# A nineteenth home for expert weights: the residual rows wait in DRAM while the experts run

## The chip, the cores and the metric

One core of one Trainium2 chip runs the whole program. The metric is device microseconds of one execution, the median of several. A profiled execution takes some microseconds longer than an unprofiled one; both times are given below. TensorE multiplies matrices, VectorE, ScalarE and GpSimd (in the profile DVE, ACT and POOL) do the rest on tiles in SBUF, and 16 DMA engines move data between DRAM and SBUF. A DMA is issued by an instruction on one of three queues: SyncE's (SP), ScalarE's (ACT) or GpSimd's (POOL). SP does nothing else here.

## The reference

256 tokens of 1024 features pass through three blocks. The first is attention and a gated convolution, and then a mixture of experts; the second and third are a gated delta rule and a forgetting attention, which are not touched by the change. What matters is the middle of the first block:

```
x = x + gt1 * y                        # residual rows, 256 x 1024 fp32 = 1 MB
h = rmsnorm(x, norm2_g) * (1 + sc2) + sh2
x = x + gt2 * hierarchical_moe(h, ...) # 32 experts, each token goes to 2 of them
x = rmsnorm(x, final_norm_g)           # and on into the second block
```

An expert has a gate and an up matrix of 1024 x 128 and a down matrix of 128 x 1024, fp32, 0.5 MB each. All 32 are read from DRAM whatever the routing: 48 MB.

## The kernel before

**Residual rows.** The tile `x` (128 partitions, 2 halves of the tokens, 1024 features; 1 MB) lives in the pool `res`. Its last writers ahead of the experts are four pieces of the output projection, `w2(0)` to `w2(3)` (line 1133), each for 256 columns: VectorE multiplies and adds (lines 1138, 1139), ScalarE squares for the norm (line 1140). After that `x` is read a last time for the routing side: TensorE transposes it (line 690), GpSimd copies columns 0 to 95 of every 128 (line 1598) and ScalarE the other 32 (line 1605) into `xp`. Nothing reads or writes `x` again until `join` (line 1877), where VectorE adds the experts' sum to it (line 1887).

**Experts.** `moe` (line 1497) splits them into eight quads of four. A quad has six loads of 1 MB: four with gate and up of one expert (two DMAs of 0.5 MB, lines 1529 and 1530), two with down of two experts (line 1536; line 1532 for the last quad). So there are 48 loads, number 6q to 6q+5 for quad q. All are issued on SP, in an order that is written out by hand. Each needs a home, a tile of 1 MB. There are 18 of them, listed in `ECYC` (line 1312): five tiles of the pool `rg` (r0 to r4), four `raw` and four `hl` tiles of the pool `wp`, and five of the block's own pool. Loads 0 to 17 get them in list order; they are issued in the order `EFIRST`, from the time when the tiles' earlier users are done, while the output projection still runs. From then on a counter walks round the list: load 18 gets the home of load 0, and so on. Two of its turns go to the gate/up and down weights of one extra tile of 32 slots, step 8 of `order`, which takes tokens that overflow their expert's 32 slots.

**Steps.** `moe_loop` (line 1747) takes the quads in the order 0, 1, 2, 3, extra, 4, 5, 6, 7, as steps i = 0 to 8. In a step `s1(i)` multiplies with gate and up (line 1333), `turn(i)` transposes, `s2(i)` multiplies with down (line 1359), and `s3(i)` adds to the sums in PSUM (lines 1377, 1378). `ahead(q)` issues the six loads of quad q some steps before they are used: quad 3 after s2(0), quads 6 and 7 after s2(4) and s2(5). SP waits in order until the home of the next load is free, that is until the matmuls that read the home's last load are done; so `s1(0)` and `s2(0)` free the homes for quad 3.

**After the experts.** `gdn` (line 1999) queues on SP, right behind the last expert load: `gfin` (0.5 MB), a weight piece `raw`, two tiles `adaA` (each 1 MB), another `raw`, two `adaX`, another `raw`. `join` computes x and its norm; in its middle it runs `fill`, the multiplication with the two `adaA` tiles (line 536), whose matmuls stand in TensorE's queue ahead of those that turn the normed rows (line 692, `dg` holds the norm's factors). TensorE, SP and ScalarE run here in the order of the program; VectorE's and GpSimd's order inside `moe` is set by a planner.

Of the kernel before, what the change touches and what calls it, by code (L numbers as in the profile page):

```python
# [12 lines left out]
F = mybir.dt.float32  # L13
# [166 lines left out]
class Kern:  # L180
# [736 lines left out]
    def block1_rest(self, pool, U, x, h, crep, u, ql, kvl, qss, kss, gq, gk, vraw, craw):  # L917
        nc, inp, const, feed, ident = self.nc, self.inp, self.const, self.feed, self.ident
# [211 lines left out]

        self.ssq4 = const.tile([128, 2, 4], F, name="ssq4")

        def w2(i):
            def ev(p):
                sl = slice(256 * i, 256 * i + 256)
                for t in range(2):
                    yt = pool.tile([128, 256], F, name="yg", tag="A2", bufs=3)
                    nc.vector.tensor_mul(yt, p[:, t, :], gt1[:, sl])
                    nc.vector.tensor_add(x[:, t, sl], x[:, t, sl], yt)
                    nc.scalar.activation(yt, x[:, t, sl], AF.Square, accum_out=self.ssq4[:, t, i:i + 1])  # L1140
                feed.chain((1.5, lambda: xt.append(self.feat_t(x, 2 * i))), (0.0, lambda: copy(i)),
                           (self.ROUTE, lambda: route(i)))
            return self.gemm_tok_g((yh, yl), 8, inp["w_out"][0], 256 * i, 256, ev)
# [4 lines left out]
        def copy(i):  # L1148
            xt[i] = (xt[i], self.sm.tile([128, 2, 256], F, name="hft", bufs=2))
            nc.vector.tensor_copy(xt[i][1], xt[i][0])  # L1150
# [150 lines left out]
    def staged(self, n, stages, us):  # L1301
# [3 lines left out]
        for r in range(n + m - 1):  # L1305
# [4 lines left out]


    ECYC = ["r4", "r0", "r1", "raw", "raw", "raw", "raw", "hl", "ex2", "ex3", "ex4", "ex0",
            "ex1", "hl", "hl", "hl", "r2", "r3"]
    EFIRST = [0, 8, 9, 10, 1, 2, 11, 12, 3, 4, 5, 6, 7, 13, 14, 15, 16, 17]
    ATT2_STEP, ORDER = 1.35, "a1b2c3"
    M0, NG, POPS = 6.0, 1, 2
# [180 lines left out]
    def moe(self, x):  # L1497
        nc, tc, inp, feed = self.nc, self.tc, self.inp, self.feed
        with tc.tile_pool(name="p2", bufs=1, reuse_waits="tile") as pool:
# [10 lines left out]
            def etile(i=None):  # L1510
                if i is None:
                    i, cnt[0] = cnt[0], cnt[0] + 1
                tag = self.ECYC[i % 18]
                return made.pop(tag) if tag in made else ering(tag)

            def ering(tag):
                pl, n = {"raw": (self.wp, self.NR), "hl": (self.wp, self.NH)}.get(
                    tag, (self.rg if tag[0] == "r" else pool, 1))
                return pl.tile([128, 2048], F, name="ew", tag=tag, bufs=n).rearrange("p (a n) -> p a n", a=2)

            cnt = [18]
            loaded, extra = {}, []

            def eload(i):

                q, s = divmod(i, 6)
                e = loaded[i] = etile(i if i < 18 else None)
                if s < 4:
                    nc.sync.dma_start(e[:, 0, :], gate[4 * q + s])
                    nc.sync.dma_start(e[:, 1, :], up[4 * q + s])  # L1530
                elif q == 7:
                    nc.sync.dma_start(by_columns(e), down[28:32, :, 512 * (s - 4):512 * (s - 4) + 512]
                                      .rearrange("e f d -> f e d"))
                else:
                    s2 = 4 * q + 2 * (s - 4)
                    nc.sync.dma_start(e, down[s2:s2 + 2].rearrange("e f d -> f e d"))
# [63 lines left out]
            with tc.manual_schedule(engines=MOE_MANUAL | {ET.DVE}):  # L1600
# [2 lines left out]
                nc.scalar.activation(warm, warm, AF.Exp)  # L1603
                for t in range(2):
                    nc.scalar.activation(xp[:, t, :, 96:128], rows[t][:, :, 96:128], AF.Copy)
                r = self.rstd_parts(self.ssq4, 1024)
                lg = T("lg", 2, 36)
                for t in range(2):
# [138 lines left out]
    def moe_loop(self, pool, x, iota, iom, rk, wk, hot, at, bw, tio, overflow, etile, quad, ahead, spare):  # L1747
        nc, tc, feed = self.nc, self.tc, self.feed
        order = [0, 1, 2, 3, 8, 4, 5, 6, 7]
        st = {q: {} for q in order}  # L1750
        xs, late = {}, {}
        xs[8] = pool.tile([128, 8, 32], F, name="xs8", bufs=1)
        ws8 = pool.tile([128, 1], F, name="ws8")

        def pair(m):

            xp = pool.tile([128, 8, 256], F, name="xs", bufs=1)
            xs[2 * m], xs[2 * m + 1] = xp[:, :, 0:128], xp[:, :, 128:256]
            n, outs = 256, [(xp, 0, 256)]
            if m == 1:  # L1760
                n, outs = 288, outs + [(xs[8], 256, 288)]
            self.gather(hot, n, outs, m == 0)
            if m < 3:
                self.picks(hot, iom, rk, m + 1)

        def weights(i):
            q = order[i]
            if q < 8:
                st[q]["w"] = quad(q)
            if q == 2:  # L1770

                gu, dn = [etile()], etile()[:, 0:1, :]
                st[8]["w"] = self.dyn_load(late["didx"], gu, dn)

        def s1(i):
            q = order[i]
            s = st[q]
            s["nt"] = 4 if q < 8 else 1
            s["hid"] = self.ffn1(pool, s["nt"], xs[q], 0, s["w"][0], self.slots[:, 8 + q:9 + q] if q < 8 else ws8,
                                 groups=[(0, 1), (2, 3)] if i == 8 else None)  # L1780

        def s2(i):
            s = st[order[i]]
            s["y"] = self.ffn2(pool, s["nt"], s["hT"], s["w"][1])

        def turn(i):
            s = st[order[i]]
            s["hT"] = self.ffn_turn(pool, s["nt"], s["hid"])

        def side(i):  # L1790

            q = order[i]
            PT = st[q]["PT"] = pool.tile([128, 256], R, name="PTs", bufs=2)
            if q < 8:
                nc.vector.tensor_scalar(PT, tio, self.slots[:, q:q + 1], None, op0=OP.is_equal)
            else:
                self.slot_side(pool, late["pw"], 0, 32, PT, ws8)

        def s3(i, *ns):
            q = order[i]  # L1800
            s = st[q]
            self.ffn3(s["nt"], s["y"], self.acc, i == 0, i == 8, s["PT"], ns)


        weights(0)
        pair(0)
        p = self.ptp()[:, :16]
        for k in range(2):
            for t in range(2):
                for g in range(4):  # L1810
                    nc.tensor.matmul(p[32 * g:32 * g + 32], at[:, k, t], bw[:, k, t, g], start=k + t == 0, stop=k + t == 2)
        self.slots = pool.tile([128, 16], F, name="slots")
        nc.vector.tensor_copy(self.slots, p)
        acc = self.acc = [[self.pmm(), self.ptp()] for _ in range(2)]
        side(0)
        tot, late["slots"], late["didx"] = overflow()
        late["pw"], _ = self.one_hots(pool, iota, 0, 32, late["slots"], wk, "8", hot[:, :, 256:288])
        s1(0)
        weights(1)
        for i in range(9):  # L1820
            if i == 0:
                s1(1)
                turn(0)
            else:
                if i > 1:
                    s1(i)
                else:
                    pair(1)
                s3(i - 1, 0)
                turn(i)  # L1830
                s3(i - 1, 1)
            if i in (1, 4):
                feed.round()
            if i == 2:

                rv = nc.values_load(tot[0:1, 0:1], min_val=0, max_val=16)
                tc.mark_branch_hint_location('spill', 'LikelyTaken', sorted(MANUAL, key=str))
            if 0 < i < 8:
                weights(i + 1)
            if i in (2, 3):  # L1840
                ahead(i + 2)
            if i < 8:
                side(i + 1)
            if i in (4, 6):
                pair((i + 1) // 2)
            if i == 4:
                self.spill(pool, rv, late["slots"], wk, iota, x, acc, spare)
            s2(i)

            if i in (0, 4, 5):  # L1850
                ahead({0: 3, 4: 6, 5: 7}[i])
        s3(8, 0, 1)
# [896 lines left out]
def build(tc, inp, out, taps=None, stop=None):  # L2749
    with ExitStack() as ctx:  # L2750
        kern = Kern(tc, ctx, inp, out, taps)
        kern.constants()
        x = kern.block1a()
        if stop != "1a":
            acc = kern.moe(x)
        if stop not in ("1a", "1"):
            kern.layer_a(acc, x)
            if stop != "2a":
                kern.layer_b(x)
        if taps is not None and stop is not None:  # L2760
            tc.nc.sync.dma_start(out.rearrange("o (t p) d -> p (o t) d", p=128), x)
# [15 lines left out]
```

## Time and profile before

| | |
|---|---|
| median of 3 runs | 861.67 us (861.54 to 864.48) |
| the profiled execution | 869.16 us, of which the span from first to last instruction is 867.3 us |
| TensorE busy | 784.4 us, 90% of the span |
| VectorE, ScalarE, GpSimd busy | 67%, 46%, 33% of the span |
| DMA | 190.25 MB, 219 GB/s over the span |
| chain that ended last | TensorE 55%, VectorE 19%, DMA 11%, of which the experts' up and down weights 7% of the span |

The shares are means over stages that differ. The experts' stage runs from about 264 us (the routing) to 375 us (the last sums of `join`); the weights begin to stream at 222 us. Of one execution 1.86 us lie outside the span.

### The profile page before, as it was taken

To read this page: it belongs to the slowest core of one execution; us is meant where nothing else is said; L and a number is where in the kernel's file an instruction comes from. 1 tells how busy PE (TensorE), PEld (TensorE's weight loads), DVE (VectorE), ACT (ScalarE), POOL (GpSimd) and SP (SyncE) were. 2 spreads that over 40 slices of the span, in tenths; PEclk is the share of its full clock that TensorE was granted. 3 is DMA by queue.
4 is the path that set the end of the run, shared out by engine and by line. 5 is a ranking of instruction groups with operands and counts; after the bars stand their busy time and mean duration, and the time that the engine had idled before them with its cause. 6 is when DMAs were issued, how large, how long until landed. Compare 5 with 4: busy or idle time off the path is not lost.

```text
span 867.3 us, 16505 instructions
## 1 busy us (share of the span) xinstructions
PE 784.4 (90%) x6595; PEld 682.5 (79%) x6595; DVE 578.2 (67%) x1168; ACT 395.6 (46%) x734; POOL 283.4 (33%) x216
## 2 busy tenths in 40 slices
PE   3889799999998999879899698998999999999986
PEld 1578688889796556468799585998998979999976
DVE  1687888854758645377588787377757458677555
ACT  2356445447334222175743244345544473544552
POOL 0144212213341200023732153124444434545433
PEclk9999999998997999989999788699999999999999
DMA  8889668889996999984353356533238756353201
GB/s 282 292 226 324 210 209 292 283 307 349 344 408 255 411 409 408 393 299 158 104 192 98 117 176 224 162 104 98 94 131 279 224 161 184 109 164 130 89 25 49
DMA packets 126325, 190.25 MB, mean 219 GB/s; under 512 B 11242, under 2 KB 84184, under 8 KB 126244
## 3 DMA queue, kind: packets, MB, share of 16 engines
q1 hardware_dynamic: 123764, 185.78, 62.0%
q10 hardware_dynamic: 1984, 1.79, 0.7%
q0 software_dynamic: 496, 1.59, 0.5%
q8 instruction: 53, 0.87, 0.4%
q14 instruction: 28, 0.23, 0.1%
HBM read 187.91 MB, written 1.22 MB: 218 GB/s over the span
## 4 chain that ended last, share of the span: by engine, by line
PE 55%; DVE 19%; DMA 11%; ACT 5%; issue 5%; POOL 3%; SPq 2%; ACTq 0%; POOLq 0%; DVEq 0%
DMA ew<-in_expert_w_up_dram 6%; PE mm L489 5%; PE mm L491 5%; PE mm L490 5%; PE mm L357 4%; PE mm L359 4%; PE mm L358 4%; PE mm L536 3%; DMA raw<-in_a_w_in_dram 2%; DVE cacc L2036 2%; DVE hl L319 2%; PE tp L1258 2%; DMA ew<-in_expert_w_down_dram 1%; PE tp L2452 1%; DVE tp L1056 1%
## 5 line engine op out<-in xcount | busy, mean ns | idle before, releaser
L319 POOL TENSOR_TENSOR hl<-raw,hl 128x1024 fp32r<-128x1024 f32 (+3 forms) x81 | 192.0, 2372 | 310.6 <-ACT hl L315 270.2
L315 ACT ACTIVATE hl<-raw 128x1024 fp32r<-128x1024 f32 (+4 forms) x156 | 153.7, 1018 | 33.2 <-DMA raw<-in_a_w_in_dram 15.5
L489 PE MATMUL mm<-h_hi,hl 128*128 128x256 f32 x448 | 136.8, 305 | 0.7 <-DVE v L946 0.4
L491 PE MATMUL mm<-h_hi,hl 128*128 128x256 f32 x448 | 130.3, 291 | 4.9 <-DVE hl L319 3.5
L490 PE MATMUL mm<-h_lo,hl 128*128 128x256 f32 x448 | 130.3, 291 | 0.2 <-DVE h_lo L706 0.2
L319 DVE TENSOR_TENSOR hl<-raw,hl 128x1024 fp32r<-128x1024 f32 (+2 forms) x75 | 97.0, 1293 | 47.6 <-ACT hl L315 45.9
L489 PEld LDWEIGHTS mm<-h_hi,hl 128*128 128x128 f32 x448 | 90.2, 201 | 6.5 <-issue 1.7
L491 PEld LDWEIGHTS mm<-h_hi,hl 128*128 128x128 f32 x448 | 89.9, 201 | 6.0 <-DVE hl L319 4.1
L490 PEld LDWEIGHTS mm<-h_lo,hl 128*128 128x128 f32 x448 | 90.1, 201 | 0.6 <-DVE h_lo L706 0.4
L357 PE MATMUL mm<-hl,h4h 128*128 128x256 f32 (+1 forms) x256 | 75.4, 295 | 1.1 <-ACT h4h L703 0.7
L358 PE MATMUL mm<-hl,h4h 128*128 128x256 f32 (+1 forms) x256 | 72.0, 281 | 0.7 <-DVE hl L319 0.7
L359 PE MATMUL mm<-hl,h4l 128*128 128x256 f32 (+1 forms) x256 | 72.0, 281 | 0.4 <-DVE h4l L706 0.2
L1056 DVE SCALAR_TENSOR_TENSOR tp<-uq,convw,tp 128x256 f32<-128x256 f32 x120 | 58.5, 487 | 3.2
L357 PEld LDWEIGHTS mm<-hl,h4h 128*128 128x128 f32 x256 | 48.2, 188 | 2.7 <-ACT h4h L703 0.9
L358 PEld LDWEIGHTS mm<-hl,h4h 128*128 128x128 f32 x256 | 48.2, 188 | 1.5 <-DVE hl L319 1.1
L2036 DVE SCALAR_TENSOR_TENSOR cacc<-mm,aconv,cacc 128x255 f32<-128x255 f32 (+2 forms) x96 | 38.7, 471 | 15.3 <-ACT cacc L2033 15.3
L359 PEld LDWEIGHTS mm<-hl,h4l 128*128 128x128 f32 x256 | 48.1, 188 | 1.0 <-DVE h4l L706 1.0
L1333 PE MATMUL tp<-ew,xs 128*32 128x256 f32 x528 | 37.6, 379 | 3.4 <-DMA ew<-in_expert_w_up_dram 3.4
L357 PE MATMUL mm<-hl,h_hi 128*128 128x256 f32 x128 | 38.2, 299 | 0.0
L1333 PEld LDWEIGHTS tp<-ew,xs 128*32 128x32 f32 x528 | 23.7, 110 | 18.0 <-issue 7.8
L358 PE MATMUL mm<-hl,h_hi 128*128 128x256 f32 x128 | 36.5, 285 | 0.2 <-POOL hl L319 0.2
L359 PE MATMUL mm<-hl,h_lo 128*128 128x256 f32 x128 | 36.3, 283 | 0.0
(681 smaller groups left out, 2000.3 us busy)
## 6 DMA issues: line engine op xcount, KB each, us to landing
raw<-in_ada_w_dram SPq DMA_DIRECT2D x30, 1024.0 KB, 8.5
raw<-in_a_w_in_dram SPq DMA_DIRECT2D x24, 1024.0 KB, 6.4
ew<-in_expert_w_gate_dram SPq DMA_DIRECT2D x32, 512.0 KB, 10.0
ew<-in_expert_w_up_dram SPq DMA_DIRECT2D x32, 512.0 KB, 11.5
ew<-in_expert_w_down_dram SPq DMA_DIRECT2D x16, 1024.0 KB, 11.7
raw<-in_b_w_in_dram SPq DMA_DIRECT2D x15, 1024.0 KB, 5.5
raw<-in_w_in_dram SPq DMA_DIRECT2D x12, 1024.0 KB, 6.5
raw<-in_a_w_out_dram SPq DMA_DIRECT2D x8, 1024.0 KB, 5.5
```

Source lines behind the costliest of these rows:

```text
L315: nc.scalar.activation(pc[2][:, ks], v[:, ks], AF.Copy)
L319: eng.tensor_tensor(pc[3][:, ks], v[:, ks], pc[2][:, ks].bitcast(F), OP.subtract)
L357: nc.tensor.matmul(pts[t], a, whi[:, k, :], start=kk == 0, stop=False)
L358: nc.tensor.matmul(pts[t], a, wlo[:, k, :], start=False, stop=False)
L359: nc.tensor.matmul(pts[t], b, whi[:, k, :], start=False, stop=kk == ko - 1)
L489: nc.tensor.matmul(p[:, b, :], wa, hh[:, kk, :], start=kk == 0, stop=False)
L490: nc.tensor.matmul(p[:, b, :], wa, hl[:, kk, :], start=False, stop=False)
L491: nc.tensor.matmul(p[:, b, :], wb, hh[:, kk, :], start=False, stop=kk == ko - 1)
L536: nc.tensor.matmul(p[32 * g:32 * g + 32, :], crep[:, hf * 4 + g, :], raws[hf][:, g, :], start=hf == 0, stop=hf == 1)
L1056: nc.vector.scalar_tensor_tensor(dst, u[:, b, tp:tp + 256], w(b, tp), dst, op0=OP.mult, op1=OP.add)
L1333: nc.tensor.matmul(pg[32 * s:32 * s + 32, :], xs[:, k, c0 + 32 * s:c0 + 32 * s + 32], gu[s][:, :, k * 128:(k + 1) * 128], start=k == 0, st ...
L2036: nc.vector.scalar_tensor_tensor(acc[:, b, sh:], p[:, b, 0:256 - sh], w(b, 3 - sh), acc[:, b, sh:], op0=OP.mult, op1=OP.add)
```

## The change

Each of the four pieces of the output projection, once it has written its 256 columns of `x`, sends them to a DRAM tile `xd` by a DMA on ScalarE's queue. The tile `x` becomes the nineteenth home, `"x"`, at the end of the list. The counter walks round 19 homes and starts at 19; load 18 (gate and up of expert 12, used in step 3) is issued on SP as soon as `x` has been read for the last time, behind ScalarE's copies in the program and ahead of the loads that follow s2(0). The home's second turn falls to load 35, down of experts 22 and 23, which s2(6) reads. At step i = 7, by when all the expert loads stand ahead of it on SP's queue, a new tile `x` takes the place of the home and is read back from `xd` in one DMA of 1 MB; `layer_a` gets this tile.

```diff
+        self.xd = self.dr.tile([128, 2, 1024], F, name="xrows", bufs=1)
         def w2(i):
             def ev(p):
...
                     nc.scalar.activation(yt, x[:, t, sl], AF.Square, accum_out=self.ssq4[:, t, i:i + 1])
+                nc.scalar.dma_start(self.xd[:, :, sl], x[:, :, sl])
...
     ECYC = ["r4", "r0", "r1", "raw", "raw", "raw", "raw", "hl", "ex2", "ex3", "ex4", "ex0",
-            "ex1", "hl", "hl", "hl", "r2", "r3"]
+            "ex1", "hl", "hl", "hl", "r2", "r3", "x"]
...
-                tag = self.ECYC[i % 18]
+                tag = self.ECYC[i % 19]
...
                 pl, n = {"raw": (self.wp, self.NR), "hl": (self.wp, self.NH), "x": (self.res, 1)}.get(
...
-            cnt = [18]
+            cnt = [19]
...
-                e = loaded[i] = etile(i if i < 18 else None)
+                e = loaded[i] = etile(i if i < 19 else None)
...
                     nc.scalar.activation(xp[:, t, :, 96:128], rows[t][:, :, 96:128], AF.Copy)
+                eload(18)
...
         for i in range(9):
+            if i == 7:
+                self.x = self.res.tile([128, 2, 1024], F, name="x")
+                nc.sync.dma_start(self.x, self.xd)
...
             acc = kern.moe(x)
+            x = kern.x
```

## Rows read from the trace of the kernel before

**Rows 1.** The page: DMA engines' busy tenths, and GB/s, in 40 slices of 21.7 us.
```profile
DMA  8889668889996999984353356533238756353201
GB/s 282 292 226 324 210 209 292 283 307 349 344 408 255 411 409 408 393 299 158 104 192 98 117 176 224 162 104 98 94 131 279 224 161 184 109 164 130 89 25 49
```

**Rows 2.** Chain of waits, the experts' end: start us, us, what.
```profile
348.67 10.21 DMA ew<-in_expert_w_up_dram
359.01 3.61 PE tp L1333 x30
```

**Rows 3.** Stretches of 4 us: busy us (count) by engine, PEclk, DMA share, GB/s.
```profile
268.00:272.00 4.00, 3.12 (x20) 2.26 (x16) 3.79 (x10) 1.47 (x3) 0.85 (x1) 0.50 0.92 322
272.00:276.00 4.00, 3.97 (x56) 3.83 (x57) 3.00 (x15) 1.77 (x4) 0.47 (x1) 0.78 0.55 224
276.00:280.00 4.00, 4.00 (x96) 4.00 (x87) 3.83 (x21) 0.44 (x2) 0.05 (x1) 1.00 0.02 6
280.00:284.00 4.00, 3.37 (x62) 2.87 (x52) 3.93 (x29) 0.23 (x1) 0.81 (x1) 1.00 0.82 280
292.00:296.00 4.00, 3.63 (x27) 1.97 (x29) 2.63 (x9) 0.89 (x3) 0.00 (x0) 1.00 1.02 411
364.00:368.00 4.00, 3.15 (x21) 0.92 (x19) 1.58 (x3) 0.63 (x1) 0.00 (x0) 1.00 1.08 364
```

**Rows 4.** Timeline of SP, DMA issues: start us, us, queue, line, destination and source.
```profile
266.92 2.09 SPq L1536 DMA_DIRECT2D ew<-in_expert_w_down_dram  x2
279.64 0.34 SPq L1529 DMA_DIRECT2D ew<-in_expert_w_gate_dram  x1
...
349.98 1.66 SPq L1532 DMA_DIRECT2D ew<-in_expert_w_down_dram  x2
...
372.05 2.14 SPq L284 DMA_DIRECT2D raw<-in_a_w_in_dram  x1
```

**Rows 5.** Timeline of ScalarE behind the last Square.
```profile
261.63 1.28 ACT L1603 ACT_TABLE_LOAD   x1
...
263.03 1.19 ACT L1605 ACTIVATE xs<-x 128x256 f32<-128x256 f32 x2
264.35 0.21 ACT L1631 ACTIVATE ge<-ge 128x8 f32<-128x8 f32 x1
```

**Rows 6.** Timeline of ScalarE and its queue at 196 us.
```profile
196.08 0.60 ACT L1096 ACTIVATE ah<-tp 128x512 fp32r<-128x512 f32 x1 [0.58 <-ACT part L539]
196.28 0.31 ACTq L583 DMA_DIRECT2D finr<-part  x1
196.69 1.28 ACT L1198 ACT_TABLE_LOAD   x1
```

**Rows 7.** Line 575, small writes to DRAM: issue ns min/median/max; issue to landing.
```profile
L575 ACTq DMA_DIRECT2D part<-part x10: 483/506/1093, 81.1 to 195.5; - x10
...
DMA to landing us min/median/max: 5.5/5.5/5.5
```

**Rows 8.** Timeline of TensorE: start us, us, line, tiles, count [idle before, releaser].
```profile
342.26 1.06 PE L1359 MATMUL mm<-ew,ehT 128*32 128x512 f32 x8
...
371.65 1.06 PE L536 MATMUL tp<-adaA,crep 128*32 128x512 f32 x8 [0.41 <-DMA adaA<-in_ada_w_dram]
374.27 1.06 PE L536 MATMUL tp<-adaA,crep 128*32 128x512 f32 x8 [1.56 <-DMA adaA<-in_ada_w_dram]
377.02 6.67 PE L692 MATMUL tp<-dg,xg 128*128 128x128 f32 x32 [1.68 <-DVE dg L1902]
```

**Rows 9.** Timeline of VectorE: the first addition of `join`.
```profile
368.70 0.68 DVE L1887 TENSOR_TENSOR x<-mm,x 128x512 f32<-128x512 f32 x1
```

**Rows 10.** Stretches of 1 us, TensorE alone: busy us (count), granted clock, DMA, GB/s.
```profile
376.00:377.00 1.00, 0.00 (x0) 0.58 1.06 379
...
382.00:383.00 1.00, 1.00 (x7) 0.51 1.03 330
383.00:384.00 1.00, 1.00 (x11) 1.00 0.66 228
```

More of the change, by code (lines that the diff above doesn't have):

```diff
@@ L1512, in etile @@
                     i, cnt[0] = cnt[0], cnt[0] + 1
-                tag = self.ECYC[i % 18]
+                tag = self.ECYC[i % 19]
                 return made.pop(tag) if tag in made else ering(tag)
             def ering(tag):
-                pl, n = {"raw": (self.wp, self.NR), "hl": (self.wp, self.NH)}.get(
+                pl, n = {"raw": (self.wp, self.NR), "hl": (self.wp, self.NH), "x": (self.res, 1)}.get(
                     tag, (self.rg if tag[0] == "r" else pool, 1))
                 return pl.tile([128, 2048], F, name="ew", tag=tag, bufs=n).rearrange("p (a n) -> p a n", a=2)
-            cnt = [18]
+            cnt = [19]
             loaded, extra = {}, []
```

## The prediction

> **What bounds the kernel now.** First the page's slices [rows 1]: TensorE is busy 90% of the span, but in slices 12 to 17 of 40 (counted from 1) the DMA digits are 9, 6, 9, 9, 9, 9, at 408, 255, 411, 409, 408 and 393 GB/s: the experts are bound by their stream of weights, which stops once, in slice 13. Then the chain of waits [rows 2]: an up matrix whose DMA was issued at 348.67 lands at 358.88, and at once the last `s1` runs; before it the chain holds only such DMAs, each issued as an earlier one lands. Then the stretches [rows 3], to see the stop: the DMA share is 0.92, 0.55, 0.02 and 0.82 in the four stretches from 268 to 284 us. Against 1 that is idle for 0.32 + 1.80 + 3.92 + 0.72 = 6.8 us, and SP's timeline says why: loads 16 and 17 are issued at 266.92 to 269.01, then nothing until 279.64 [rows 4]. All 18 homes are full and `s1(0)` has yet to free one. From there the stream runs at 411 GB/s [rows 3] without a gap.
>
> What comes behind the stream decides how much of an earlier end is kept. SP goes on from the last expert load at 349.98 to 351.64 with 7.5 MB (gfin 0.5, three raw, two adaA, two adaX) until 374.19 [rows 4], and the DMA share stays above 1. So the engines are busy up to about 385 us, by the same queue. In TensorE's timeline [rows 8] the multiplication with the first adaA waits 0.41 us for its DMA, that with the second 1.56 us, to 374.27; then L692 waits 1.68 us for the norm's factors, to 377.02. Two paths run nearly level here: the sums of `join` (368.70 [rows 9] up to L692), and the bytes up to the second adaA.
>
> **The change, step by step.**
>
> *The home filled in the stop.* Load 18 is 1 MB: 1.049 MB / 411 GB/s = 2.55 us. If it lies in the stop, 29 loads are left behind it instead of 30, so the last up matrix lands at 358.88 - 2.55 = 356.33. The start of the rest is unchanged: it hangs on s1(0) and s2(0), whose weights are in homes long before. The later loads find their homes as early as now: each turn round the list comes one load later, and a load is issued some 10 us ahead of its landing (348.67 to 358.88 [rows 2]), so the queue stays full.
>
> *Four writes to DRAM.* 1 MB more, 2.6 us at 408 GB/s [rows 1], while the engines are full (slice 12). The loads behind move back by as much, into the stop. The trace has no write of this size. Below: nothing less than zero, since nothing is taken out. Above: twice the time, 5.1 us, if a write goes at half the rate; I know no row nearer than the tail's 364 GB/s at a share of 1.08 with pieces of short runs [rows 3], which gives 2.9 us. I take 2.6. With load 18 that fills 2.6 + 2.55 = 5.15 of 6.8 us; at 5.1 us the sum is 7.65 and 0.85 us of the gain is lost.
>
> *When the home is free.* GpSimd's copies of x are done earlier, ScalarE's end at 264.22 [rows 5]; the fourth write goes out at about 261.6. A write of 8 KB in the loaded stretch at 270 us took 5.5 us to land [rows 7]; so 267.1. SP is in order and has loads 16 and 17 until 269.01 [rows 4]: load 18 follows at 269.0. Bounds for the landing of a 256 KB write: below, no time at all (261.6); above, 5.5 and 3 x 0.64 us for the three writes ahead of it, 7.4, that is 269.0. Only behind 269.0 would it hold SP, where the next load waits until 279.64 anyway. So 10 us of cover.
>
> The Trainium skill, page "DMA: Bandwidth & Descriptors", section "Anatomy of one DMA", speaks against this step: a DMA counts as done only when its last byte is confirmed in the target, which is slowest into HBM. By its fit of 2.0 us + bytes / 436 GB/s a write of 256 KB lands after 2.6 us (an estimate of that page), at 264.2, by the row after 5.5 us; both are ahead of 269.0, so the sum is the same, and the chance of the rival "the home comes free too late" is small.
>
> *The issues on ScalarE.* Three of the four stand where ScalarE waits for VectorE next. The fourth stands ahead of the table load at 261.63. From there to 264.22 ScalarE is without a gap, and `ge`, on the chain to the routing, starts at 264.35 [rows 5]: 0.13 us of slack. Issues at this kind of place take 0.48 to 1.09 us [rows 7]. But an issue can run beside the engine: at 196.28 one of 0.31 us lies inside an activation of 0.60 and the next instruction starts at 196.69, without delay [rows 6]. The last Square and its read-out give 0.5 us of such cover. So 0 to 1.0 us; I take 0.2, near the row that shows cover.
>
> *The read back.* 1 MB on SP behind load 47, 2.55 us at 411 GB/s, 2.9 at 364 [rows 3]. Its home is free: s2(6), at 342.26 to 344.2 [rows 8], is over before SP gets there at about 349.1 (351.64 - 2.55). What stands behind it on SP is gfin, raw, adaA, adaX; `join` and `fill` wait for those. Up to the second adaA the queue holds as many bytes as before, one load less and one read more. So adaA lands as now, at 371.65 and 374.27. x itself: the last down matrix lands 2 MB behind the up matrix, 5.1 us, so at 361.4 now; x at 364.0. `join` wants it at 368.70 - 2.55 = 366.15 [rows 9]: 2.1 us to spare.
>
> *What is kept.* The sums of `join` come 2.55 us earlier, so dg would let L692 start at 374.5. But `fill` stands ahead of it: 374.27 + 1.06 = 375.33 [rows 8]. L692 starts at 375.35 instead of 377.02. Gain 1.67 us of the 2.55; adaA is late next. Behind L692 ScalarE and TensorE carry one chain, with weights that landed long before for the first two jobs; I let the 1.67 pass through to the end.
>
> Sum: -1.67 + 0.2 = -1.5 us, rounded. The profiled execution of 869.16 us would become 867.7; it lies 7.5 us above the median of the runs, 861.67, and I take the difference over as it is: 860.2 us.
>
> **The rivals.**
>
> *Nothing moves* (861.7, from 861.2 to 862.2). VectorE's order is a planner's, and behind 385 us other waits may take the 1.5 us. For it: the two paths into L692 are only 1.67 us apart. Against: TensorE starts L692 late by the norm alone.
>
> *The clock gives more* (857.5). The granted clock falls to half, 1.2 of 2.4 GHz, at about 376 and is back at 1.00 behind 383 [rows 10], after TensorE stood idle between `fill` and L692; L692 takes 6.67 us [rows 8] and at the full clock would take half, 3.3. If the shorter wait keeps the clock up, the gain is 1.5 + 3.3 = 4.8, and in between if the clock falls for less of L692; I give 4.2 as the middle, 857.5. Against: TensorE's work is the same, and it now waits 0.41 + 2.55 = 3.0 us ahead of the first adaA, so the clock may fall as well, only sooner.
>
> The Trainium skill, page "TensorE: Matmul & The Clock Gate", section "HAM oscillation — how this bites in real kernels", has it that waits for DMA between bursts of matmuls throttle TensorE: by that rule the longer wait for adaA lowers the clock too, and this rival gives nothing beyond the 1.5. Here the clock falls behind waits of 0.41, 1.56 and 1.68 us [rows 8, 10], of which two are for DMAs; so the rule keeps the rival's chance low.
>
> *The home comes free too late* (slower, 866.0). One mechanism: the writes land late, so load 18 misses the stop and stands on SP ahead of quad 3. Then nothing is saved in the stream, and the read back puts 2.6 us of bytes ahead of adaA: adaA at 376.8, L692 at 377.9 at least, and every us that SP stands behind 279.64 comes on top. A write that lands at 283 gives 0.9 + 3.4 = +4.3, 866.0. It decides from where load 18 is issued behind some 275 us, 281 less the 5.5 us from issue to landing of [rows 7]. Against: it can go out at 269.0, and the write that it waits for has 7 us to land.
>
> *The tail gives it back* (slower by little, 862.5). The read of what was just written runs at half the rate: 5.1 us in place of 2.55, adaA at 376.8, L692 at 377.9 instead of 377.02, so +0.9. No row shows a read from DRAM at that rate.
>
> **How the numbers follow.** Forecast -1.5 (between -0.5 and -2.6): 0.50. Nothing moves: 0.19. The clock: 0.16, some 0.1 of it beyond 4.3 us. Home too late: 0.07, most of it beyond 4.3, since nothing bounds the hold on SP. The tail: 0.08. About 0.5%, 4.3 us, is what a measurement of this kernel can tell from no change. Faster by more: 0.10, slower by more: 0.06, the rest 0.84. The forecast alone has 859.1 to 861.2; it reaches down to the clock's middle, 857.5, and up past the writes' and issues' upper ends (860.2 + 0.85 + 0.8 = 861.9) and the tail (862.5) to 863.2, 0.7 more for the spread of the runs, of which the median lies 0.1 above the lowest and 2.8 below the highest. That leaves out the rest of the clock and the late home, under 2 in 10.
>
> **What would show it.** The idle stretch from 274 to 281 us shrinks to under 2 us, the stream's last up matrix lands near 356.5, L692 starts near 375.5 right behind `fill` and no longer waits for dg. SP issues load 18 at 269 to 270. Wrong would be: a load 18 behind 275, ge behind 264.7, adaA's second half behind 375, x as the last wait of the first addition, or another length of the half clock behind 376.

## The result and the profile after: 2.7% slower

The changed kernel takes 885.23 us (median of 4 runs, 883.18 to 886.02); the kernel before beside it takes 861.61 us (4 runs, 861.26 to 864.48). The ratio is 1.0266, with an interval of 1.0232 to 1.0300. A second set gave 884.59 against 862.49, ratio 1.0284 (1.0237 to 1.0332). The forecast was 860.2 us. The profiled execution of the changed kernel took 883.18 us, span 881.3, which is 2 us under its median; that of the kernel before lies 7.5 us above its own. So a profiled execution is not always the longer one: in this study they lie between 4 us under and 11 us above the median of their kernel, and the whole times of two profiles can't be set against each other. The traces are compared up to 400 us. There the changed kernel is 22 us late, close to the 23.6 us between the medians; why the profile of the kernel before lost some 8 us behind that is open.

Start with the page's slices of the changed kernel: DMA tenths and GB/s, in 40 slices of 22.0 us.
```profile
DMA  8889668889549999997435166633247755454201
GB/s 283 287 225 326 218 219 292 280 317 332 193 143 375 409 408 409 408 385 257 146 111 177 48 225 209 192 96 96 97 144 256 248 170 159 130 152 136 97 25 48
```
In [rows 1] slices 11 and 12 carry 344 and 408 GB/s, and the stop is in slice 13 with 255. Now slices 11 and 12 have 193 and 143, and slice 13 has 375. The stop is filled, but a much larger hole has opened ahead of it, from 220 to 264 us. The next two views, one of each kernel, size it by stretches: busy us (count) by engine, PEclk, DMA share, GB/s. First the kernel before, in a stretch that was not read for the prediction:
```profile
222.00:240.00 18.00, 16.13 (x128) 13.60 (x128) 11.93 (x17) 6.60 (x9) 4.83 (x2) 1.00 1.00 388
240.00:260.00 20.00, 20.00 (x176) 19.99 (x174) 10.61 (x18) 6.86 (x16) 8.87 (x8) 1.00 1.03 410
260.00:276.00 16.00, 12.21 (x101) 8.11 (x101) 12.65 (x51) 10.15 (x20) 2.20 (x4) 0.68 0.88 333
276.00:290.00 14.00, 12.47 (x187) 10.14 (x175) 11.68 (x57) 2.23 (x6) 4.85 (x5) 1.00 0.68 258
```
and then the changed kernel:
```profile
222.00:240.00 18.00, 16.13 (x129) 13.60 (x127) 12.13 (x17) 6.39 (x9) 4.83 (x2) 1.00 0.61 234
240.00:260.00 20.00, 19.90 (x174) 19.78 (x172) 11.03 (x19) 7.08 (x16) 8.80 (x8) 1.00 0.34 120
260.00:276.00 16.00, 12.31 (x103) 8.31 (x105) 12.71 (x51) 10.41 (x20) 2.26 (x4) 0.68 0.79 299
276.00:290.00 14.00, 6.83 (x66) 3.41 (x61) 7.34 (x49) 0.40 (x2) 0.00 (x0) 0.78 1.03 409
```
Up to 276 us the missing bytes are 18 x 154 + 20 x 290 + 16 x 34 = 9.1 MB, at 409 GB/s 22.3 us. From 276 to 290 the stream gets 14 x 151 = 2.1 MB back, which is 5.2 us, because the stop is gone. Of what has moved by then 1.05 MB (2.6 us) are the writes and no weights. So the weights should be 22.3 - 5.2 + 2.6 = 19.7 us late, and they are. TensorE's timeline of the changed kernel (start us, us, line, tiles, count, [idle before, releaser]):
```profile
378.89 3.61 PE L1336 MATMUL tp<-ew,xs 128*32 128x256 f32 x30 [1.52 <-DMA ew<-in_expert_w_up_dram]
394.50 1.94 PE L536 MATMUL tp<-adaA,crep 128*32 128x512 f32 x8 [3.20 <-DMA adaA<-in_ada_w_dram]
397.12 1.94 PE L536 MATMUL tp<-adaA,crep 128*32 128x512 f32 x8 [0.69 <-DMA adaA<-in_ada_w_dram]
398.99 5.83 PE L692 MATMUL tp<-dg,xg 128*128 128x128 f32 x32
```
The last up matrix is 19.9 us later than in [rows 2]; the second adaA, behind the read back as well, is 22.9 us later than in [rows 8]. L692 starts without a wait right behind `fill`, 22.0 us later.

Why did the stream stop? SP's queue tells it. These are its waits in the changed kernel (line, waited for: us in total, times, longest):
```profile
SPq L1539 <- DMA xrows<-x: 14.6, 1, 14.6
SPq L1533 <- DMA xrows<-x: 8.9, 1, 8.9
SPq L1532 <- DMA xrows<-x: 5.1, 1, 5.1
SPq L1589 <- DMA xrows<-x: 4.3, 1, 4.3
```
Lines 1532, 1533 and 1539 load gate, up and down of experts; line 1589 loads `gt2r`. None of them has anything to do with `x` in DRAM, yet four of them stood 32.9 us for the four writes. ScalarE's queue and SP's, side by side in time (the first fence is ScalarE's, the second SP's, both of the changed kernel):
```profile
241.04 0.59 ACTq L1143 DMA_DIRECT2D xrows<-x  x1
247.54 0.55 ACTq L1143 DMA_DIRECT2D xrows<-x  x1
255.45 0.52 ACTq L1143 DMA_DIRECT2D xrows<-x  x1
260.95 0.52 ACTq L1143 DMA_DIRECT2D xrows<-x  x1
```
```profile
229.73 0.33 SPq L1533 DMA_DIRECT2D ew<-in_expert_w_up_dram  x1
244.69 0.38 SPq L1539 DMA_DIRECT2D ew<-in_expert_w_down_dram  x1
250.25 0.33 SPq L1532 DMA_DIRECT2D ew<-in_expert_w_gate_dram  x1
259.48 0.33 SPq L1533 DMA_DIRECT2D ew<-in_expert_w_up_dram  x1
264.17 0.33 SPq L1589 DMA_DIRECT2D gt2r<-row  x1
```
Each of the four SP issues behind the first row comes 2.7 to 4.0 us after a write goes out, and the waits above name the writes as what they ended with. In the kernel before, gt2r goes out at 229.99.

The compiled program says what ties them: the semaphores on which these DMA issues wait (number on the queue, line, DMA, its waits). A completion semaphore is a counter that a DMA raises when it has landed; `DMAHW0` to `DMAHW7` are eight of them, and `PE` stands for a wait for TensorE. Before, SP's issues:
```
94  L1529 gate [DMAHW0,PE]   95 L1530 up [DMAHW1]     96 L1529 gate [DMAHW2]   97 L1530 up [DMAHW3]
98  L1529 gate [DMAHW4,PE]   99 L1530 up [DMAHW5]    100 L1536 down [DMAHW6]
101 L1529 gate [DMAHW7,PE]  102 L1530 up [DMAHW0]    103 L1586 gt2r [DMAHW1]
```
After, SP's issues and ScalarE's four writes:
```
94  L1532 gate [DMAHW0,PE]   95 L1533 up [DMAHW1]     96 L1532 gate [DMAHW6]   97 L1533 up [DMAHW7]
98  L1532 gate [DMAHW0,PE]   99 L1533 up [DMAHW1]    100 L1539 down [DMAHW2]
101 L1532 gate [DMAHW3,PE]  102 L1533 up [DMAHW4]    103 L1589 gt2r [DMAHW5]
ScalarE: L1143 xrows [DMAHW2]   [DMAHW3]   [DMAHW4]   [DMAHW5]
```
The DMAs of SP and of ScalarE share eight completion semaphores, dealt in turn. The instruction records of the traces show the same: in this stretch the DMAs of SP and ScalarE raise semaphores 101, 102, 103, 105 and 107 to 110, always in this order by the program's plan, the four writes 103, 105, 107 and 108, and GpSimd's DMAs raise others, from 111 on. Before a DMA is issued, its queue waits until the DMA that held the same semaphore before has landed. The program's plan sets the four writes between SP's issues 95 and 96, long before they can run, so numbers 2 to 5 pass through them, and the next four SP issues that get these numbers (100 to 103) each wait for one write, hence for `w2(0)` to `w2(3)`.

The kernel before had the same rule in its waits, as waits of a load for a DMA that it has no use for. So SP waits for more than a free home, which is all that the description of the kernel before names (SP's waits, same columns):
```profile
SPq L1530 <- DMA ew<-in_expert_w_up_dram: 11.4, 12, 1.6
SPq L1530 <- DMA ew<-in_expert_w_down_dram: 10.9, 5, 2.2
```

### The profile page after: what moved, and what is told of

Its sections match the earlier page's. It is cut to its first block, busy times and chain, and to the rows that moved or that the text cites. A ratio compares the mean times of both kernels' runs of the same rounds, so it can differ in the third digit from the quotient of the medians.

```text
span 881.3 us, 16515 instructions
## 1 busy us (share of the span) xinstructions
PE 786.9 (89%) x6595; PEld 674.8 (77%) x6595; DVE 577.8 (66%) x1168; ACT 396.0 (45%) x734; POOL 283.1 (32%) x216
## 4 chain that ended last, share of the span: by engine, by line
PE 34%; DVE 13%; DMA 4%; ACT 3%; POOL 3%; issue 2%; SPq 1%; POOLq 0%; ACTq 0%; DVEq 0%
PE mm L358 3%; PE mm L357 3%; PE mm L359 3%; PE mm L489 2%; PE mm L490 2%; PE mm L491 2%; DVE cacc L2044 2%; DMA adaA<-in_ada_w_dram 1%; DMA ew<-in_expert_w_gate_dram 1%; PE tp L2460 1%; DVE NU L2259 1%; PE tp L1336 1%; DVE zb L2426 1%; SPq L526 1%; DMA raw<-in_a_w_in_dram 1%
## 5 line engine op out<-in xcount | busy, mean ns | idle before, releaser
L489 PE MATMUL mm<-h_hi,hl 128*128 128x256 f32 x448 | 134.0, 299 | 0.7 <-DVE v L946 0.4
L491 PE MATMUL mm<-h_hi,hl 128*128 128x256 f32 x448 | 128.1, 286 | 5.0 <-DVE hl L319 3.5
L490 PE MATMUL mm<-h_lo,hl 128*128 128x256 f32 x448 | 127.9, 286 | 0.2
L489 PEld LDWEIGHTS mm<-h_hi,hl 128*128 128x128 f32 x448 | 87.2, 195 | 6.4 <-issue 1.7
L491 PEld LDWEIGHTS mm<-h_hi,hl 128*128 128x128 f32 x448 | 87.4, 195 | 6.1 <-DVE hl L319 4.1
L490 PEld LDWEIGHTS mm<-h_lo,hl 128*128 128x128 f32 x448 | 87.4, 195 | 0.7 <-DVE h_lo L706 0.6
L1336 PE MATMUL tp<-ew,xs 128*32 128x256 f32 x528 | 45.7, 422 | 15.8 <-DMA ew<-in_expert_w_up_dram 15.7
```

The lines of the kernel that those rows point to most:

```text
L489: nc.tensor.matmul(p[:, b, :], wa, hh[:, kk, :], start=kk == 0, stop=False)
L490: nc.tensor.matmul(p[:, b, :], wa, hl[:, kk, :], start=False, stop=False)
L491: nc.tensor.matmul(p[:, b, :], wb, hh[:, kk, :], start=False, stop=kk == ko - 1)
L1336: nc.tensor.matmul(pg[32 * s:32 * s + 32, :], xs[:, k, c0 + 32 * s:c0 + 32 * s + 32], gu[s][:, :, k * 128:(k + 1) * 128], start=k == 0, st ...
```

## The experiments

Theory **T** (turns): the loss is SP standing in its turn behind a write that is planned early and runs late. Its rivals: **B**, the bytes of the writes or their landing in DRAM slow the reading; **H**, the home (load 18, its wait, the read back) holds SP. The first four ran beside 19 runs of the kernel before (861.15 us median, 857.7 to 866.1), the others beside 29 (862.49, 855.47 to 866.06).

**A write of 1 KB behind `w2(3)`, nothing else.** The kernel before and one small write on ScalarE; no home, no read back.
```diff
+        self.xd = self.dr.tile([1, 1024], F, name="xrows", bufs=1)
...
+                if i == 3:
+                    nc.scalar.dma_start(self.xd[:, sl], x[0:1, 0, sl])
```


> The kernel before, and one write of 1 KB (one partition, 256 columns of x) on ScalarE's queue behind the Square of w2(3), at about 261 us; no home, no read back. Theory T (turns): SP's and ScalarE's DMAs take eight completion semaphores in turn, in the order of the program's plan, and each waits until the DMA that had its semaphore before has landed. Here gt2r is the next DMA on the write's semaphore, so SP stands at gt2r until about 263.5 us, where it had stood at 230; five expert loads are out by then and the rest come behind, as in the changed kernel. T expects 880 to 885 us. Theory B (bytes: the 1 MB of writes is what costs, by its traffic or by slow writes to DRAM): 1 KB costs nothing, 861.5. Theory H (the home and the read back cost it): neither is there, 861.5.

878.79 us (877.36 to 889.39, 5 runs), ratio 1.0186 (1.0148 to 1.0224). One wait and its place in SP's timeline:
```profile
SPq L1590 <- DMA xrows<-x: 33.7, 1, 33.7
```
```profile
230.75 0.33 SPq L1534 DMA_DIRECT2D ew<-in_expert_w_up_dram  x1
264.82 0.33 SPq L1590 DMA_DIRECT2D gt2r<-row  x1
```
```profile
240.00:260.00 20.00, 20.00 (x174) 20.00 (x173) 10.60 (x18) 6.86 (x16) 8.95 (x8) 1.00 0.01 2
```
A transfer of 1 KB stops the stream for 20 us and more: 2 GB/s from 240 to 260, in the view by stretches. T said 880 to 885, whose lower end is 1.2 us too high; the rivals said no change. B and H are out as the main cause: neither the bytes nor the home are there, and three quarters of the loss (17.6 of 23.6 us) are.

**The same 1 KB behind `w2(0)`.** The diff is that of the run above with `if i == 0:`.

> As the kernel with one 1 KB write, but behind w2(0), at about 241 us. T: SP stands at gt2r until 243 us and then goes on. The five loads before it are through by about 235.5 (5 MB at 409 GB/s from 222), so the DMA engines stand idle for some 9 us, and the stop of 6.8 us before s1(0) takes most of it back: 2 to 4 us, 863.5 to 866. B and H: 861.5.

863.25 us (858.89 to 866.37, 10 runs), ratio 1.0011 (0.9984 to 1.0037): no change that can be told. T had said 863.5 to 866, the rivals 861.5, so the time alone does not part them; the wait does.
```profile
SPq L1590 <- DMA xrows<-x: 11.9, 1, 11.9
```
gt2r goes out at 244.72. The hold is there, but it ends 20 us earlier, and little of it is left: counted from `ge`, the start of the routing, L692 is 1.2 us later than before, where the write behind `w2(3)` makes it 18.4 us later. So what counts is when the write can run, not that there is one. That the queue's backlog and the stop of 6.8 us take up the rest is T's account, and it fits; no run takes the stop away to show it.

**The four full writes alone.** The kernel before with the change's tile `xd` and its line 1143; 18 homes, no read back.
```diff
+        self.xd = self.dr.tile([128, 2, 1024], F, name="xrows", bufs=1)
...
+                nc.scalar.dma_start(self.xd[:, :, sl], x[:, :, sl])
```


> The kernel before with the change's four writes of 256 KB on ScalarE's queue and nothing else: 18 homes, x stays in its tile. T: SP is held at four loads by the four writes as in the changed kernel, 882 to 886; the read back that is missing gives up to 2.6 us back. B: 864 to 885, by how slow the writes are. H: 861.5 to 862, since neither home nor read back is there.

878.34 us (878.2 to 886.1, 4 runs), ratio 1.0215 (1.0156 to 1.0275), a few us under what T expected. SP's waits on the writes are those of the changed kernel within 1.2 us each (15.8, 8.3, 5.3, 4.1), and L692 starts at
```profile
394.75 5.87 PE L692 MATMUL tp<-dg,xg 128*128 128x128 f32 x32 [0.69 <-DVE dg L1905]
```
That is 4.2 us ahead of the changed kernel. But this profile runs 1.9 us ahead from the first write on (239.15 where the changed kernel has 241.04), so 2.3 us are left, and they fit the read of 1 MB that is missing in front of adaA (2.55 us by the forecast's rate). By its ratios the changed kernel is 0.5 to 0.7% (4 to 6 us) above this one, with intervals that overlap. The later L692 would cover 2.3 us of that; the rest is within what the intervals leave open, and no run separates it further.

**The change with one write on GpSimd's queue.** All of the change but line 1143; in its place one write of 1 MB behind the norm's rstd, with GpSimd in program order in that stage.
```diff
-                nc.scalar.dma_start(self.xd[:, :, sl], x[:, :, sl])
...
-            with tc.manual_schedule(engines=MOE_MANUAL | {ET.DVE}):
+            with tc.manual_schedule(engines=MOE_MANUAL | {ET.DVE, ET.Pool}):
...
-                eload(18)
                 r = self.rstd_parts(self.ssq4, 1024)
+                nc.gpsimd.dma_start(self.xd, x)
+                eload(18)
```


> The changed kernel, with x written by one DMA of 1 MB on GpSimd's queue behind the norm factors (about 263.5 us) in place of the four on ScalarE's; GpSimd runs in the program's order there. Home, load 18 and read back as in the change. GpSimd's DMAs have other semaphores than SP's and ScalarE's. T: SP runs as in the kernel before, and what was forecast for the change comes out: 859.5 to 862.5, load 18 issued at about 270 us. B: the same 1 MB is written, 883 to 885. H: home and read back are still there, 883 to 885.

860.08 us (854.65 to 863.18, 10 runs), ratio 0.9980 (0.9952 to 1.0008): the whole loss is gone. SP waits for this write at load 18, until 271.11, and nowhere else:
```profile
SPq L1531 <- DMA xrows<-x: 2.8, 1, 2.8
```
The stream is full up to the stop, and the stop is mostly filled: 2.5 us idle in place of 6.8 (view by stretches, to be set beside [rows 3]):
```profile
268.00:272.00 4.00, 3.08 (x14) 2.81 (x14) 3.95 (x10) 0.62 (x2) 0.62 (x1) 0.50 1.01 415
272.00:276.00 4.00, 4.00 (x68) 3.87 (x71) 2.99 (x10) 2.17 (x4) 0.53 (x1) 0.88 1.03 412
276.00:280.00 4.00, 4.00 (x81) 4.00 (x76) 3.80 (x27) 0.28 (x1) 0.00 (x0) 1.00 0.40 149
280.00:284.00 4.00, 3.19 (x51) 2.34 (x46) 3.43 (x25) 0.28 (x1) 0.00 (x0) 1.00 0.97 369
```
and its tail, in TensorE's timeline:
```profile
355.43 3.61 PE L1335 MATMUL tp<-ew,xs 128*32 128x256 f32 x30 [1.51 <-DMA ew<-in_expert_w_up_dram]
370.52 1.93 PE L536 MATMUL tp<-adaA,crep 128*32 128x512 f32 x8 [2.88 <-DMA adaA<-in_ada_w_dram]
373.16 1.93 PE L536 MATMUL tp<-adaA,crep 128*32 128x512 f32 x8 [0.71 <-DMA adaA<-in_ada_w_dram]
375.02 5.62 PE L692 MATMUL tp<-dg,xg 128*128 128x128 f32 x32
```
This profile runs 0.8 us ahead of the one before from 222 us on. Without that the last up matrix is 2.8 us earlier and L692 1.2 us.

**The change with only the queue exchanged.** The four writes stay in their places and go out on GpSimd's queue.
```diff
-                nc.scalar.dma_start(self.xd[:, :, sl], x[:, :, sl])
+                nc.gpsimd.dma_start(self.xd[:, :, sl], x[:, :, sl])
```


> The change with one word exchanged: the same four writes of 256 KB at the same places, issued on GpSimd's queue instead of ScalarE's. T: GpSimd's DMAs don't take a turn with SP's and ScalarE's completion semaphores, so SP waits for no write until load 18 (issued 269 to 273 us); gate and up of expert 1 and gt2r go out at 229 to 231 us as before the change, and the time is that of the kernel with one GpSimd write, 858 to 862 us. Rival H, the writes or their bytes cost by themselves: 878 or more, as with the writes alone on ScalarE's queue. Rival G, GpSimd stands on each write's issue (0.8 us each) and its halves of the weights' split come late: up to 4 x 0.8 us, 863 to 864.

865.98 us (862.88 to 870.18, 12 runs), ratio 1.0045 (1.0020 to 1.0069). The changed kernel on the same chip took 884.59. One word takes back 18.6 us of the 22.1 that were lost. SP has no wait for a write, and gt2r goes out at 231.91, in a profile that runs 1.9 us late from 196 us on, so no later than before the change. The rest lies on GpSimd, as rival G had it, but not where G named it: not in the issues (0.7 to 0.95 us each) but in what stands behind them. GpSimd's timeline here:
```profile
256.50 0.68 POOL L1143 DMA_DIRECT2D xrows<-x  x1 [2.21 <-DVE x L1141]
263.49 0.68 POOL L1143 DMA_DIRECT2D xrows<-x  x1 [6.30 <-DVE x L1141]
264.06 0.30 POOL L1595 IOTA iota<- 128x32 f32 x1
264.58 3.16 POOL L1601 COPY xs<-x 128x768 f32<-128x768 f32 x2
268.14 0.72 POOL L621 TENSOR_TENSOR rstd<-rstd,pexp 128x2 f32<-128x2 f32 x1
```

GpSimd is in order, so its copies into `xp` and the rstd stand behind the fourth write, which waits for `w2(3)`. In the kernel with one write the same rows stood at
```profile
252.54 1.78 POOL L1600 COPY xs<-x 128x768 f32<-128x768 f32 x1 [0.56 <-DVE x L1141]
254.66 1.66 POOL L1600 COPY xs<-x 128x768 f32<-128x768 f32 x1 [0.35 <-DVE x L1141]
...
261.92 0.70 POOL L621 TENSOR_TENSOR rstd<-rstd,pexp 128x2 f32<-128x2 f32 x1
262.57 0.82 POOL L1609 DMA_DIRECT2D xrows<-x  x1
```
`ge`, on the chain to the routing, starts 5.9 us after ScalarE's table load instead of 2.7 [rows 5]:
```profile
263.81 1.28 ACT L1606 ACT_TABLE_LOAD   x1
269.74 0.21 ACT L1635 ACTIVATE ge<-ge 128x8 f32<-128x8 f32 x1 [0.63 <-DVE ge L1634]
```
That is 3.2 us of routing. By its ratio this kernel is 0.45% (3.9 us) above the kernel before and 0.65% (5.6 us) above the one with a single GpSimd write, so the routing is the larger part of either; no run shows where the remainder goes.

**The tail: adaA ahead of the weight piece.** As the kernel with one GpSimd write waits for adaA, its tail was tried with the two adaA tiles ahead of the first `raw`.
```diff
-        feed.add(gq[0])
         fill.todo = fill.load()
+        feed.add(gq[0])
```


> The kernel with one GpSimd write (860.1 us), and the two adaA tiles queued ahead of the first weight piece of the next layer instead of behind it (0.5 MB or 1 MB less ahead of them). T's view of the tail (the bytes up to adaA set the start of L692 once the experts end earlier): the wait for adaA shrinks by 2.5 us, dg is late next (373.8 us there), L692 starts about 1.2 us earlier and the time is 858.5 to 859. Rival (the two paths behind it are level, another wait takes it): 860. Rival (the weight piece is late now): 861.

860.57 us (855.45 to 863.55, 12 runs), ratio 0.9984 (0.9956 to 1.0011). The wait changed as T said: L692 waits 2.76 us for dg, `fill` only 0.23 us for the second adaA, and counted from `ge` L692 starts 1.5 us earlier than without the swap. The time shows nothing of it that can be told from 0.9980, and T's 858.5 to 859 was not reached. Level paths behind L692 take it, or it is under the spread; which of the two is open.

**The same swap in the kernel before.**

> The kernel before with the same swap of adaA and the weight piece alone. There L692 waits for dg (1.68 us), not for adaA, so T: no change, 861 to 862 us. Rival (the bytes up to adaA bound the kernel before already): 859 to 860, as much as in the kernel with the GpSimd write.

864.2 us (859.08 to 870.33, 12 runs), ratio 1.0028 (1.0000 to 1.0056): no gain, as expected, and if anything a small loss, 2 us above what T gave. There L692 waits 2.67 us for dg and starts as long after `ge` as without the swap (112.7 us), so the swap only makes `fill` end sooner.

**The changed kernel once more**, as the yardstick of that session:

> The changed kernel once more, beside the three others. Turns (T): 883 to 886 us as in its first run, with SP standing about 33 us on the four writes. If its loss over the kernel with the writes alone (878.3) was a difference of two sessions: about 879.

884.59 us (880.86 to 893.07, 6 runs), SP's four waits 15.1, 7.9, 5.2 and 4.7 us. No kernel of this study beats the kernel before by more than can be told.

## Why the prediction was wrong, step by step

*Four writes to DRAM* is the step that failed. It charged the writes their 2.6 us of bytes and let the loads behind move into the stop. The bytes were nearly right: with one write and load 18 the stop kept 2.5 us of 6.8, a use of 4.3 where I had 5.15. What was missing is that a write on ScalarE's queue stands in one turn with SP's loads. It took four issues of SP, 32.9 us of standing and 22 us of stream. The prediction asked whether the *landing* of the writes would hold load 18, and which instructions stand behind the issue on ScalarE; both are fair questions and neither is the point. *The chain of waits* says that each DMA was "issued as an earlier one lands"; I took that for the depth of one queue and never asked which earlier one, though SP's waits of the kernel before name it.

*When the home is free*, and its rival "the home comes free too late": neither decided. Load 18 went out at 291.97, where 269 to 270 was forecast and a start behind 275 was the sign of being wrong (the first row below, SP's timeline of the changed kernel). But it waited for no write itself; all that stood ahead of it was late. Load 10, the fourth that SP issues, was the first to be held. The price of a landing was also taken from another queue: the 5.5 us of [rows 7] belong to a write that GpSimd issues, which that view lists below the ten of ScalarE (second row, the kernel before), and the fit that was set beside it (the Trainium skill, page "DMA: Bandwidth & Descriptors", section "Anatomy of one DMA") is given there for DMAs that GpSimd issues. ScalarE's four writes let SP go after 2.7 to 4.0 us.
```profile
291.97 0.34 SPq L1532 DMA_DIRECT2D ew<-in_expert_w_gate_dram  x1
```
```profile
L575 POOL DMA_DIRECT2D part<-part x1: 850/850/850, 269.8 to 269.8; - x1
```

*The home filled in the stop* holds where the stream is full: 2.8 us earlier with the GpSimd write, for 2.55 predicted. In the changed kernel it is worth nothing: the stream is 20 us late and has no stop there, a DMA share of 1.03 from 276 to 290 us.

*The issues on ScalarE* (0.2 us): ScalarE shows 0.26 and 0.21 us ahead of the activations behind the first two, and `ge` starts at 264.15 where it was 264.35 [rows 5], in a profile that runs 0.2 us ahead at `w2(0)`. So no cost shows.

*The read back* and *What is kept* hold too, by the trace. In the kernel with one GpSimd write adaA is late next, with waits of 2.88 and 0.71 us where I had worked out 3.0 for the first; L692 stands behind `fill`, 1.2 us earlier (1.67 predicted). Its ratio says -0.2% (-0.5 to +0.1%), and -1.5 us is -0.17%; the interval holds no change as well, so the time alone does not confirm it. The forecast describes that kernel and not this one.

*"The clock gives more"* did not come: with the write on GpSimd the granted clock is 0.50 from 369 to 378 us, before the change from about 376 to 383 [rows 10]. It falls sooner, as the text argued against this rival, and it stays down some 3 us longer. The fall before the change does not hang on the waits alone, though. In the kernel with 1 KB behind `w2(3)` the waits ahead of L692 are 0.50, 1.58 and 1.56 us, much as in [rows 8]; the granted clock stays at 1.00 from 392 to 404 us, and L692 takes 3.84 us in place of 6.67:
```profile
398.03 3.84 PE L692 MATMUL tp<-dg,xg 128*128 128x128 f32 x32 [1.56 <-DVE dg L1906]
```

No rival had the mechanism. The chance of 0.06 for slower was carried by load 18 alone, and the hold on SP that "nothing bounds" was put behind the write of the home, not behind any write planned ahead of the loads.

## What to carry to other kernels

Before a DMA is added, ask in which turn it stands: whose issues wait for its completion semaphore, and when it can run at the latest. An early place in the plan with a late source is the costly case, whatever the size, and a queue that doesn't share the turn avoids it, if what stands behind the issue on that engine can wait. In a profile of before, a load's issue that waits for a DMA whose data it does not use is the sign. Not tried here: the same writes on ScalarE's queue, but planned behind the expert loads.

## What the runs showed of the hardware that was not expected

- A write of 1 KB on ScalarE's queue kept SP from issuing for 33.7 us and cost 17.6 us; the same write 20 us earlier cost nothing that can be told.
- DMAs issued by GpSimd did not take part in that turn: SP had no wait for any of the four, and only load 18, which overwrites the tile that the write reads, waited for the single one (2.8 us).
- A write of 1 MB on GpSimd's queue took 8.4 us from issue to landing beside a full stream, and the four of 256 KB there 6.0 to 7.2 us; four of 256 KB on ScalarE's queue let SP go 2.7 to 4.0 us after their issue while the stream was nearly empty.
